# Input stage of a hybrid decoder layer: order of the low weight parts, shared value weights, rows of triangular blocks dealt in turn

## The chip, the cores and the metric

The kernel runs on one core of a Trainium2 chip. The metric is the device time of one execution in microseconds. The core has a matrix engine (TensorE, PE in the profile, with PEld for its weight loads), a vector engine (VectorE, DVE), an activation engine (ScalarE, ACT), GpSimd (POOL), and a queue for DMA issues (SyncE, SP). Each engine executes its own list of instructions in order; semaphores tie the lists together.

## The reference

One layer on 1024 tokens of width 1024: a norm, an input projection, two mixers side by side (sparse attention, and a gated delta rule with 4 heads of 128), an output projection, a gated feed-forward part with a short convolution. The change lies in the delta-rule mixer's input:

```python
h = rmsnorm(x, norm_mix[l])
proj = h @ w_in[l]
q_nsa, kv_nsa, gate_nsa, qkv_gdn, z_gdn, b_gdn, a_gdn = jnp.split(proj, SPLIT_POINTS, axis=-1)
...
qkv = jax.nn.silu(causal_dwconv(qkv, conv_w))
q, k, v = jnp.split(qkv, 3, axis=-1)
...
a_mat = jnp.where(strict, jnp.einsum('nbhid,nbhjd->nbhij', kb, kc) * decay, 0.0)
eye = jnp.eye(c, dtype=jnp.float32)
rhs = jnp.concatenate([vb, kb * jnp.exp(gcum)[..., None]], axis=-1)
sol = lax.linalg.triangular_solve(a_mat + eye, rhs, left_side=True, lower=True, unit_diagonal=True)
```

The chunks have 64 tokens. All is in float32; the kernel keeps the accuracy in its matmuls by splitting each operand in a high and a low part and adding three products: high by high, high by low, low by high.

## The kernel before

**Projection.** The normed input lies transposed in SBUF as `hH` and `hL`, [128, 8, 1024] each: 8 slices k of the model width by 1024 tokens. `split_weight` loads a [128, 1024] weight (512 KB, L113), ACT copies the high part `w_h` (L116), POOL subtracts to get the low part `w_l` (L118). `proj_block` makes one block of 128 output columns by 512 tokens: for each k the three matmuls of `mm3`, `w_h` by `hH` (L126), `w_h` by `hL` (L127), `w_l` by `hH` (L128), 24 in all, into one of two result banks `proj_ps`. The page prints the operands with the moving one first, `proj_ps<-hH,w_l`.

**Convolution.** `conv_block(ct, b)` serves column block ct (0 to 3 queries, 4 to 7 keys, 8 to 11 values, one head each) and half b of the tokens. ACT copies the bank to `cv_raw` and, scaled by a tap, to `cv_acc`; VectorE adds the three other taps (L465); ACT takes a tanh, VectorE finishes the silu (L469), and a DMA stores 512 tokens to `d_kqv` (L470). The last three columns of half 0 are kept in `tail` for half 1 (L460, L457). The loop in `phase_in` runs ct 0 to 11 for half 0, then ct 0 to 11 for half 1, and each call splits its own weight: 24 splits.

**Triangular blocks.** For a pair p of 128-token tiles `gdn_pre` loads `kq` (512 KB in 1024 pieces of 512 B, L276), makes the Gram products `kk_ps` (L285) and stores the 32 by 32 diagonal blocks of the strictly triangular matrix to `d_blk` (L297). `gdn_blocks` loads all 32 blocks of the pair as `bb`, [128, 32, 32], with each block in four partitions (L342), and inverts them there on VectorE: a partition holds one block and 8 of the 32 rows of its solution, `zb`. In 31 steps a multiply (L348) and an add (L350) apply one column of the block to the first `na` of the 8 rows. Partition 4i + r holds rows 8r to 8r + 7; since the same instruction runs on all partitions, `na` must cover the partition with the most rows that have begun, and so is `min(8, j + 1)`. The result goes to `d_z` (L352) in pieces of 1 KB. `gdn_solve` reads it back in transposed order, four loads of 16 KB a tile (`Zx`, L365), and puts blocks together on TensorE. `gdn_scale`, `gdn_scan` (L408, L415, L419) and `gdn_out` (L437 to L445) follow per tile.

**What sets the order.** The code of the delta rule stands behind the convolution loop in the text but has a raised priority, and a scheduler merges it with the convolution blocks, the blocks of `z` (gate of the delta rule) and the compressed keys (`kc_ps`, L704) into one fixed list for each engine. A list is executed in order, SP's DMA issues too. About 430 us into the execution the input stage is over, and the attention and the feed-forward part follow.

Of the kernel before, what the change touches and what calls it, by code (L numbers as in the profile page):

```python
# [9 lines left out]
F32 = mybir.dt.float32  # L10
# [8 lines left out]
P = 128  # L19
# [3 lines left out]
NK = DM // P  # L23
# [23 lines left out]
def shape_constants():  # L47
# [10 lines left out]
    c[:, C_DM:C_DM + 64] = j[:, None] == np.arange(64)[None, :]  # L58
    rho = i % 4
    for a in range(8):  # L60
        c[i, C_ZI + a * 32 + 8 * rho + a] = 1.0
    k = np.arange(P)
# [128 lines left out]
def proj_block(K, w, b):  # L191

    wh, wl = w
    ps = K.pp.tile([P, 512], F32, name="proj_ps", tag="proj")
    d = slice(b * 512, (b + 1) * 512)
    mm3(K.nc, ps, [(wh[:, k * P:(k + 1) * P], wl[:, k * P:(k + 1) * P], K.hH[:, k, d], K.hL[:, k, d])
                   for k in range(NK)])
    return ps
# [138 lines left out]
def gdn_blocks(K, p):  # L337

    nc = K.nc
    db, dz = K.d_blk[p % 2], K.d_z[p % 2]  # L340
    bb = K.gt.tile([P, 32, 32], F32, name="bb", tag="bb")
    nc.sync.dma_start(bb, bc(db.rearrange("t b h j i -> (t b h) j i"), 1, 4))  # L342
    z = K.gt.tile([P, 8, 32], F32, name="zb", tag="zb")
    nc.vector.tensor_copy(z, K.zinit)
    for j in range(31):
        na, n = min(8, j + 1), 31 - j
        tmp = K.gt.tile([P, 8, 32], F32, name="ztmp", tag="ztmp", bufs=1)
# [3 lines left out]
                                op=ALU.add)  # L351
    nc.sync.dma_start(dz.rearrange("t b h (r a) i -> (t b h r) (a i)", a=8), z.rearrange("p a i -> p (a i)"))  # L352


def gdn_solve(K, t, st):

    nc = K.nc
    B, wq, keg, vv = st.B, st.wq, st.keg, st.vv
    dz = K.d_z[t // 2 % 2][t % 2]
    Z, zt, qs = K.Zx[t % 2], K.zt, K.qs  # L360
    for c in range(2):
        nc.gpsimd.memset(Z[64 * c:64 * c + 32, :, 64 * c + 32:64 * c + 64], 0.0)
    for b in range(4):
        d = slice(32 * b, 32 * b + 32)
        nc.sync.dma_start(Z[d, :, d], dz[b].rearrange("h r i -> r h i"))  # L365

# [80 lines left out]

def conv_block(K, ct, b):

    nc = K.nc  # L450
    which, h = ct // 4, ct % 4
    ps = proj_block(K, split_weight(K, K.A["w_gdn"][ct]), b)
    raw = K.scr.tile([P, 3 + 512], F32, name="cv_raw", tag="cv_raw")
# [55 lines left out]
def phase_in(K, ctx):  # L509
# [45 lines left out]
    with ExitStack() as st:  # L555
# [15 lines left out]
        for b in range(2):  # L571
            gdn_gates(K, b)
        for ct in range(12):
            conv_block(K, ct, 0)
        for ct in range(12):
            conv_block(K, ct, 1)
        cp = mk("cmp", 1)
# [842 lines left out]
def open_common(K, ctx):  # L1420
# [35 lines left out]
    K.d_blk = [dp.tile([2, 4, 4, 32, 32], F32, name=f"d_blk{i}") for i in range(2)]  # L1456
    K.d_z = [dp.tile([2, 4, 4, 32, 32], F32, name=f"d_z{i}") for i in range(2)]

# [88 lines left out]
```

## Time and profile before

| | us |
|---|---|
| median of three runs | 1500.3 (1497.18, 1500.30, 1500.89) |
| the profiled execution | 1502.3 |
| its span in the trace | 1500.5 |
| TensorE busy | 1420.9 (95%) |
| VectorE busy | 1153.7 (77%) |
| ScalarE busy | 723.3 (48%) |
| GpSimd busy | 575.3 (38%) |

The span is what the trace covers; 1.8 us of the execution lie outside it. The share of busy time is an average over stages with different limits. Busy time of TensorE is modelled at its ends, so it is read beside the clock that the chip granted: 1.00 is 2.4 GHz, and a stretch with a mean below it spent part of its time at the lower level of 1.2 GHz. In groups of instructions the two numbers behind the bar are busy us and mean ns of one; behind the next bar stands how long the engine sat idle just before them, and what ended it. Groups are shown by the line that issued them.

### The profile page before, as it was taken

Reading aid. Unit: us, or ns where it says so; the run is one execution under the profiler, and the core shown is the slowest. Engines: PE = TensorE matmul, PEld = TensorE weight load, DVE = VectorE, ACT = ScalarE, POOL = GpSimd, SP = SyncE. Lnnn points to the kernel's source line nnn. Section 1 sums busy time; section 2 is a strip of 40 time slices with the busy share of each in tenths; the row PEclk is TensorE's granted clock in tenths of the full one; section 3 lists DMA queues with packets and bytes.
Section 4 is the critical chain, followed back from the end, with each engine's and each line's share of the span. In section 5 each row is a group of like instructions: output and inputs, shape, how many; then the busy total and the mean of one; then the engine's idle time right before and its main releaser. Section 6 shows DMA issues by size and latency. Waiting matters only on the chain.

```text
span 1500.5 us, 21074 instructions
## 1 busy us (share of the span) xinstructions
PE 1420.9 (95%) x7260; PEld 1163.8 (78%) x7260; DVE 1153.7 (77%) x2222; ACT 723.3 (48%) x1405; POOL 575.3 (38%) x567
## 2 busy tenths in 40 slices
PE   8998899999989999989998979999999999989997
PEld 8876677787877777777787858888888888778886
DVE  5768997886335788898975797888888888687656
ACT  7443343232233566788865544444444445333333
POOL 3355433344352245466563541111111112364444
PEclk9999999999999999999999989999999999999999
DMA  6245352444366543132215112323222235773333
GB/s 234 87 156 177 107 169 72 125 121 150 93 219 173 161 138 112 58 85 52 55 64 200 40 70 105 105 105 106 105 94 98 97 105 194 268 267 87 103 106 147
DMA packets 106059, 188.04 MB, mean 125 GB/s; under 512 B 17216, under 2 KB 52064, under 8 KB 105952
## 3 DMA queue, kind: packets, MB, share of 16 engines
q1 hardware_dynamic: 105952, 186.69, 38.5%
q8 instruction: 57, 0.93, 0.3%
q14 instruction: 50, 0.41, 0.1%
HBM read 135.00 MB, written 51.66 MB: 124 GB/s over the span
## 4 chain that ended last, share of the span: by engine, by line
PE 64%; DVE 19%; DMA 6%; ACT 4%; issue 4%; POOL 2%; SPq 1%; DVEq 0%; ACTq 0%; POOLq 0%
PE up_ps L1130 27%; PE dn_ps L1328 11%; PE proj_ps L128 3%; PE proj_ps L126 3%; PE proj_ps L127 3%; DVE cv_acc L465 3%; PE pt L880 2%; DVE pl L890 2%; PE po L892 1%; DVE zb L350 1%; PE po L891 1%; DVE ztmp L348 1%; PE s_ps L820 1%; PE s_ps L415 1%; DMA d_x<-og 1%
## 5 line engine op out<-in xcount | busy, mean ns | idle before, releaser
L1328 PE MATMUL dn_ps<-d_op 128*128 128x512 f32 x924 | 211.4, 390 | 5.7 <-DVE d_op L1322 3.8
L1328 PEld LDWEIGHTS dn_ps<-d_op 128*128 128x128 f32 x924 | 173.0, 188 | 43.6 <-DVE d_op L1322 5.0
L128 PE MATMUL proj_ps<-hH,w_l 128*128 128x512 f32 x384 | 158.3, 412 | 6.6 <-POOL w_l L118 6.6
L126 PE MATMUL proj_ps<-hH,w_h 128*128 128x512 f32 x384 | 156.2, 408 | 5.0 <-ACT cv_acc L463 3.2
L127 PE MATMUL proj_ps<-hL,w_h 128*128 128x512 f32 x384 | 155.3, 405 | 0.1
L1320 POOL TENSOR_TENSOR d_op<-a_raw,d_op 128x1024 fp32r<-128x1024 f32 (+1 forms) x42 | 104.7, 2496 | 123.0 <-ACT d_op L1319 105.6
L1130 PE MATMUL up_ps<-th,op_h 128*128 128x512 f32 x336 | 133.5, 398 | 7.1 <-ACT op_h L1154 7.1
L1130 PE MATMUL up_ps<-th,op_l 128*128 128x512 f32 x336 | 133.6, 398 | 3.6 <-DVE op_l L1156 3.6
L1130 PE MATMUL up_ps<-tl,op_h 128*128 128x512 f32 x336 | 133.3, 397 | 0.0
L118 POOL TENSOR_TENSOR w_l<-w_raw,w_h 128x1024 fp32r<-128x1024 f32 (+2 forms) x46 | 110.1, 2398 | 46.1 <-ACT w_h L116 44.5
L1322 DVE TENSOR_TENSOR d_op<-b,d_op 128x1024 fp32r<-128x1024 f32 (+1 forms) x42 | 80.8, 1928 | 48.5 <-ACT d_op L1321 42.1
L1130 PE MATMUL up_ps<-dl,op_h 128*128 128x512 f32 x288 | 113.8, 395 | 0.0
L1130 PE MATMUL up_ps<-dh,op_h 128*128 128x512 f32 x288 | 112.6, 395 | 1.0 <-ACT acc L167 1.0
L1130 PE MATMUL up_ps<-dh,op_l 128*128 128x512 f32 x288 | 110.5, 394 | 0.0
L882 ACT ACTIVATE ph<-pt 128x512 fp32r<-128x512 f32 (+1 forms) x148 | 85.3, 591 | 49.1 <-PE pt L880 41.3
L1242 DVE SCALAR_TENSOR_TENSOR ga<-f_g,vec,ga 128x1024 f32<-128x1024 f32 x44 | 89.3, 2029 | 16.9 <-ACT ga L1240 16.3
L890 DVE TENSOR_TENSOR pl<-pt,ph 128x512 fp32r<-128x512 f32 x132 | 89.5, 683 | 9.1 <-ACT ph L882 8.6
L128 PEld LDWEIGHTS proj_ps<-hH,w_l 128*128 128x128 f32 x384 | 74.6, 194 | 26.9 <-POOL w_l L118 10.6
L1154 ACT ACTIVATE op_h<-w_raw 128x1024 fp32r<-128x1024 f32 (+1 forms) x64 | 59.0, 923 | 74.8 <-PE up_ps L1130 69.7
L1319 ACT ACTIVATE d_op<-a_raw 128x1024 fp32r<-128x1024 f32 (+1 forms) x42 | 41.4, 988 | 108.7 <-PE dn_ps L1328 53.8
L1175 POOL MEMSET f_u<- 128x2 f32 x22 | 2.2, 100 | 234.0 <-DVE acc L1242 233.1
L126 PEld LDWEIGHTS proj_ps<-hH,w_h 128*128 128x128 f32 x384 | 74.6, 195 | 21.2 <-ACT cv_acc L463 4.9
(343 smaller groups left out, 3654.6 us busy)
## 6 DMA issues: line engine op xcount, KB each, us to landing
w_raw<-in_w_up_dram SPq DMA_DIRECT2D x44, 512.0 KB, 3.2
a_raw<-d_a SPq DMA_DIRECT2D x35, 512.0 KB, 3.6
w_raw<-in_w_gdn_dram SPq DMA_DIRECT2D x24, 512.0 KB, 3.5
d_a<-ga SPq DMA_DIRECT2D x44, 256.0 KB, 2.0
b<-in_w_down_dram SPq DMA_DIRECT2D x20, 512.0 KB, 6.9
d_a<-so SPq DMA_DIRECT2D x33, 256.0 KB, 2.0
qT<-d_q SPq DMA_DIRECT2D x32, 256.0 KB, 4.8
mg<-d_mix SPq DMA_DIRECT2D x16, 512.0 KB, 3.7
```

What stands on the lines that cost most here:

```text
L118: (low or nc.gpsimd).tensor_tensor(out=wl, in0=raw, in1=wh.bitcast(F32), op=ALU.subtract)
L126: nc.tensor.matmul(out, ah, bh, start=(i == 0), stop=False)
L127: nc.tensor.matmul(out, ah, bl, start=False, stop=False)
L128: nc.tensor.matmul(out, al, bh, start=False, stop=(i == n - 1))
L882: nc.scalar.activation(ph[0:kk], pt[0:kk], AF.Copy)
L890: nc.vector.tensor_tensor(out=pl, in0=pt, in1=ph.bitcast(F32), op=ALU.subtract)
L1130: mm = lambda a, b, start, stop: nc.tensor.matmul(out, a, b, start=start, stop=stop, skip_group_check=not first)
L1154: nc.scalar.activation(h, src, AF.Copy)
L1242: nc.vector.scalar_tensor_tensor(out=a, in0=raw[:, j:j + SEQ], scalar=tap(j), in1=a, op0=ALU.mult, op1=ALU.add)
L1320: nc.gpsimd.tensor_tensor(out=al, in0=raw, in1=ah.bitcast(F32), op=ALU.subtract)
L1322: nc.vector.tensor_tensor(out=bl, in0=b[js.start], in1=bh.bitcast(F32), op=ALU.subtract)
L1328: one = lambda a, b, start, stop: nc.tensor.matmul(ps, a, b, start=start, stop=stop, skip_group_check=not first)
```

## The change

1. `proj_block` no longer calls `mm3`. It issues the 16 matmuls with `w_h` first (`hH`, `hL` for each k in turn) and the 8 with `w_l` last, all from one line (L199).
2. `conv_block` gets the split weight. The loop now runs queries and keys of half 0, then the values of both halves with one split for the two, then queries and keys of half 1: 20 splits in place of 24.
3. In the triangular blocks partition 32r + i (r = 0 to 3) holds block i and rows r, r + 4, r + 8, ... of its solution, so `na` is `j // 4 + 1`. The initial values (C_ZI) follow this, `bb` is loaded by four DMAs of 32 partitions, and `d_z` has the rows first, [32, 2, 4, 4, 32], so that its store has pieces of 128 B. The loads of `Zx` have the same pieces as before.

```diff
-    rho = i % 4
+    rho = i // 32
     for a in range(8):
-        c[i, C_ZI + a * 32 + 8 * rho + a] = 1.0
+        c[i, C_ZI + a * 32 + 4 * a + rho] = 1.0
...
-    mm3(K.nc, ps, [(wh[:, k * P:(k + 1) * P], wl[:, k * P:(k + 1) * P], K.hH[:, k, d], K.hL[:, k, d])
-                   for k in range(NK)])
+
+    jobs = [(wh, h, k) for k in range(NK) for h in (K.hH, K.hL)] + [(wl, K.hH, k) for k in range(NK)]
+    for n, (w, h, k) in enumerate(jobs):
+        K.nc.tensor.matmul(ps, w[:, k * P:(k + 1) * P], h[:, k, d], start=(n == 0), stop=(n == len(jobs) - 1))
...
-    nc.sync.dma_start(bb, bc(db.rearrange("t b h j i -> (t b h) j i"), 1, 4))
+    for r in range(4):
+        nc.sync.dma_start(bb[32 * r:32 * r + 32], db.rearrange("t b h j i -> (t b h) j i"))
...
-        na, n = min(8, j + 1), 31 - j
+        na, n = j // 4 + 1, 31 - j
...
-    nc.sync.dma_start(dz.rearrange("t b h (r a) i -> (t b h r) (a i)", a=8), z.rearrange("p a i -> p (a i)"))
+    nc.sync.dma_start(dz.rearrange("(a r) t b h i -> (r t b h) a i", r=4), z)
...
-    dz = K.d_z[t // 2 % 2][t % 2]
+    dz = K.d_z[t // 2 % 2][:, t % 2]
...
-        nc.sync.dma_start(Z[d, :, d], dz[b].rearrange("h r i -> r h i"))
+        nc.sync.dma_start(Z[d, :, d], dz[:, b])
...
-def conv_block(K, ct, b):
+def conv_block(K, ct, b, w):
...
-    ps = proj_block(K, split_weight(K, K.A["w_gdn"][ct]), b)
+    ps = proj_block(K, w, b)
...
-        for ct in range(12):
-            conv_block(K, ct, 0)
-        for ct in range(12):
-            conv_block(K, ct, 1)
+
+        for cts, bs in ((range(8), (0,)), (range(8, 12), (0, 1)), (range(8), (1,))):
+            for ct in cts:
+                w = split_weight(K, A["w_gdn"][ct], low=None)
+                for b in bs:
+                    conv_block(K, ct, b, w)
...
-    K.d_z = [dp.tile([2, 4, 4, 32, 32], F32, name=f"d_z{i}") for i in range(2)]
+    K.d_z = [dp.tile([32, 2, 4, 4, 32], F32, name=f"d_z{i}") for i in range(2)]
```

On the engines' lists the change shows so. From the start of the attention on, the lists of all engines are the same before and after. Line numbers behind L199 are some 2 to 5 higher in the changed kernel.

TensorE at the compressed keys, before. `kc_ps` is the key product, `proj_ps` the block of another projection that fills in, `ot_ps` the output transposes, `s_ps` the state product of the scan, for which VectorE makes `vn`; x4 is four in a row.

```order
L408 MATMUL m_ps<-S,wq 128x128 x2
L704 MATMUL kc_ps<-cmp_x,w_4040 64x128
L126 MATMUL proj_ps<-hH,w_h 128x512
L127 MATMUL proj_ps<-hL,w_h 128x512
L437 MATMUL ot_ps<-ident,vv 128x128 x4
L415 MATMUL s_ps<-vn,kt 128x128 x4
L419 MATMUL o_ps<-vn,ab 128x128 x4
L704 MATMUL kc_ps<-cmp_x,w_4040 64x128
L128 MATMUL proj_ps<-hH,w_l 128x512
```

The same place after; six more pairs of `proj_ps` stand where the row of dots is.

```order
L411 MATMUL m_ps<-S,wq 128x128
L709 MATMUL kc_ps<-cmp_x,w_4028 64x128
L199 MATMUL proj_ps<-hH,w_h 128x512
L199 MATMUL proj_ps<-hL,w_h 128x512
...
L440 MATMUL ot_ps<-ident,vv 128x128 x4
L199 MATMUL proj_ps<-hH,w_h 128x512
L199 MATMUL proj_ps<-hL,w_h 128x512
L440 MATMUL ot_ps<-ident,vv 128x128 x4
L418 MATMUL s_ps<-vn,kt 128x128 x4
L422 MATMUL o_ps<-vn,ab 128x128 x4
L709 MATMUL kc_ps<-cmp_x,w_4028 64x128
L199 MATMUL proj_ps<-hH,w_l 128x512 x2
```

All 16 high-part matmuls of the block now stand between the first key product and `s_ps`, where two stood; the low-part ones come behind.

GpSimd about the end of the convolution's first half, before (`tail` and `cv_raw` are the three kept columns, `wq` and `sm` belong to the delta rule).

```order
L460 COPY tail<-cv_raw 128x3
L455 MEMSET cv_raw 128x3
L118 TENSOR_TENSOR w_l<-w_raw,w_h 128x1024
L460 COPY tail<-cv_raw 128x3
L455 MEMSET cv_raw 128x3
L333 TENSOR_TENSOR wq<-kq,gb 128x4x128
L118 TENSOR_TENSOR w_l<-w_raw,w_h 128x1024
L460 COPY tail<-cv_raw 128x3
L455 MEMSET cv_raw 128x3
L323 TENSOR_TENSOR sm<-sm,phalf 128x4
L118 TENSOR_TENSOR w_l<-w_raw,w_h 128x1024
```

The same place after.

```order
L463 COPY tail<-cv_raw 128x3 x2
L460 COPY cv_raw<-tail 128x3
L458 MEMSET cv_raw 128x3
L335 TENSOR_TENSOR wq<-kq,gb 128x4x128
L118 TENSOR_TENSOR w_l<-w_raw,w_h 128x1024
L335 TENSOR_TENSOR wq<-kq,gb 128x4x128
L325 TENSOR_TENSOR sm<-sm,phalf 128x4
L463 COPY tail<-cv_raw 128x3
L460 COPY cv_raw<-tail 128x3
L403 TENSOR_TENSOR ab<-at,cst 128x512
L335 TENSOR_TENSOR wq<-kq,gb 128x4x128
...
L118 TENSOR_TENSOR w_l<-w_raw,w_h 128x1024
```

One subtraction now serves two value blocks, and work of the delta rule stands between the subtractions.

SyncE's issues about the end of the convolution, before, from the last weight of the convolution (`in_w_gdn`); `kq_2578` and `kq_2605` are the loads of two tiles of the second half, `vT` one of values.

```order
L113 DMA w_raw_1765<-in_w_gdn_dram 128x1024
L113 DMA w_raw_1811<-in_w_z_dram 128x1024
L276 DMA kq_2578<-d_kqv_88 128x8x128
L470 DMA d_kqv_88<-cv_th_1675 128x512
L113 DMA w_raw_1875<-in_w_z_dram 128x1024
L317 DMA vT_2462<-d_kqv_88 128x4x128
L470 DMA d_kqv_88<-cv_th_1718 128x512
L113 DMA w_raw_1939<-in_w_z_dram 128x1024
L470 DMA d_kqv_88<-cv_th_1761 128x512
L276 DMA kq_2605<-d_kqv_88 128x8x128
```

The same place after (the rows ahead are stores and weights).

```order
L319 DMA vT_2444<-d_kqv_88 128x4x128
L473 DMA d_kqv_88<-cv_th_1694 128x512
L113 DMA w_raw_1915<-in_w_z_dram 128x1024
L473 DMA d_kqv_88<-cv_th_1737 128x512
L113 DMA w_raw_1979<-in_w_z_dram 128x1024
L319 DMA vT_2743<-d_kqv_88 128x4x128
L473 DMA d_kqv_88<-cv_th_1780 128x512
L278 DMA kq_2560<-d_kqv_88 128x8x128
L278 DMA kq_2587<-d_kqv_88 128x8x128
L509 DMA d_z_act_90<-z_th_1818 128x512
```

The first `kq` of the second half stood three stores ahead of the last `d_kqv`; now both stand behind it. Next on this list come the solution's store and eight loads of `Zx`.

## Rows read from the trace of the kernel before

**Rows 1.** The page, busy us of each engine, share, and number of instructions.

```profile
PE 1420.9 (95%) x7260; PEld 1163.8 (78%) x7260; DVE 1153.7 (77%) x2222; ACT 723.3 (48%) x1405; POOL 575.3 (38%) x567
```

**Rows 2.** Stretches of the span, with their length, busy time, and granted clock.

```profile
core 0: us, PE busy (x) PEld busy (x) DVE busy (x) ACT busy (x) POOL busy (x), PEclk, DMA share, GB/s
70.00:95.00 25.00, 25.00 (x110) 20.20 (x110) 16.42 (x17) 10.95 (x21) 12.28 (x12) 1.00 0.36 121
95.00:150.00 55.00, 49.29 (x221) 37.63 (x220) 44.50 (x78) 22.71 (x46) 32.42 (x29) 0.94 0.57 179
150.00:215.00 65.00, 59.02 (x301) 45.66 (x300) 61.85 (x150) 25.96 (x55) 26.69 (x20) 0.95 0.42 130
215.00:350.00 135.00, 131.84 (x916) 108.22 (x915) 108.94 (x330) 43.98 (x125) 47.81 (x47) 1.00 0.41 120
350.00:360.00 10.00, 7.50 (x30) 6.01 (x30) 7.08 (x14) 4.56 (x15) 7.84 (x8) 0.67 0.49 136
```

**Rows 3.** TensorE by lines, 95 to 215 us: count, busy, mean, idle before.

```profile
L128 PE MATMUL proj_ps<-hH,w_l 128*128 128x512 f32 x126 | 53.7, 426 | 6.6 <-POOL w_l L118 6.6
L126 PE MATMUL proj_ps<-hH,w_h 128*128 128x512 f32 x126 | 52.2, 415 | 3.2 <-ACT cv_acc L463 3.2
L127 PE MATMUL proj_ps<-hL,w_h 128*128 128x512 f32 x126 | 51.5, 408 | 0.0
```

**Rows 4.** TensorE in order of time: start us, us, instruction, idle before.

```profile
138.16 0.71 PE L128 MATMUL proj_ps<-hH,w_l 128*128 128x512 f32 x1 [2.13 <-POOL w_l L118]
138.67 0.63 PE L126 MATMUL proj_ps<-hH,w_h 128*128 128x512 f32 x1
139.10 0.63 PE L127 MATMUL proj_ps<-hL,w_h 128*128 128x512 f32 x1
```

**Rows 5.** VectorE in order of time, a held and an undisturbed instruction.

```profile
141.83 2.49 DVE L348 TENSOR_TENSOR ztmp<-zb,bb 128x112 f32<-128x112 f32 x1
...
144.88 0.74 DVE L465 SCALAR_TENSOR_TENSOR cv_acc<-cv_raw,vec,cv_acc 128x512 f32<-128x512 f32 x1
```

**Rows 6.** GpSimd in order of time at the same place.

```profile
141.79 2.39 POOL L118 TENSOR_TENSOR w_l<-w_raw,w_h 128x1024 fp32r<-128x1024 f32 x1 [1.97 <-ACT w_h L116]
```

**Rows 7.** VectorE by lines, 95 to 215 us, columns as in the third group.

```profile
L465 DVE SCALAR_TENSOR_TENSOR cv_acc<-cv_raw,vec,cv_acc 128x512 f32<-128x512 f32 x48 | 50.9, 1061 | 7.9 <-ACT cv_acc L463 6.0 <-POOL wq L333 1.4
L348 DVE TENSOR_TENSOR ztmp<-zb,bb 128x112 f32<-128x112 f32 (+29 forms) x43 | 21.2, 493 | 0.5
L350 DVE TENSOR_TENSOR zb<-zb,ztmp 128x112 f32<-128x112 f32 (+29 forms) x42 | 18.6, 442 | 0.7
```

**Rows 8.** GpSimd's subtraction, 95 to 215 us: shortest, median, longest ns; starts.

```profile
L118 POOL TENSOR_TENSOR w_l<-w_raw,w_h x16: 2347/2396/2943, 96.6 to 210.6; 128x1024 fp32r<-128x1024 f32 x16
```

**Rows 9.** VectorE by lines and shapes, 135 to 350 us.

```profile
L348 DVE TENSOR_TENSOR ztmp<-zb,bb 128x192 f32<-128x192 f32 x4 | 1.4, 355 | 0.0
...
L348 DVE TENSOR_TENSOR ztmp<-zb,bb 128x8 f32<-128x8 f32 x4 | 0.7, 171 | 0.1
```

**Rows 10.** DMA issues, 95 to 235 us: size of one, median us to landing.

```profile
d_kqv<-cv_th SPq DMA_DIRECT2D x18, 256.0 KB, 2.2
kq<-d_kqv SPq DMA_DIRECT2D x6, 512.0 KB, 5.5
...
d_blk<-B SPq DMA_DIRECT2D x16, 16.0 KB, 1.7
d_z<-zb SPq DMA_DIRECT2D x2, 128.0 KB, 2.8
```

**Rows 11.** TensorE in order of time at the compressed keys.

```profile
349.98 0.60 PE L437 MATMUL ot_ps<-ident,vv 128*128 128x128 f32 x4
353.08 1.88 PE L415 MATMUL s_ps<-vn,kt 64*128 64x128 f32 x8 [2.50 <-DVE vn L409]
```

**Rows 12.** The stores of the convolution: issue ns, first and last start.

```profile
L470 SPq DMA_DIRECT2D d_kqv<-cv_th x24: 319/320/433, 53.9 to 224.2; - x24
```

**Rows 13.** TensorE in order of time, the Gram products of the fifth tile.

```profile
232.36 1.09 PE L285 MATMUL kk_ps<-kq 128*64 128x128 f32 x16
```

## The prediction

> **What bounds the kernel now.** The first view is the page: TensorE is busy 95% of the span and VectorE 77% [rows 1], so a microsecond counts only where TensorE stands or runs at the lower of its two clock levels. Next is the order of instructions of the two kernels. From about 430 us on it is the same on every engine (the last 4700 of 6763 TensorE and 1461 of 2224 VectorE instructions), so only the input stage can move. The third view is the table by stretches [rows 2]. From 70 to 95 us 110 matmuls fill 25.00 us without a gap at a granted clock of 1.00, which is 0.227 us for one of 512 columns. From 95 to 215 us, where convolution blocks, triangular blocks and weight splits lie together, TensorE is busy 49.29 of 55 and 59.02 of 65 us, at a clock of 0.94 and 0.95. There VectorE is busy 61.85 of 65 us: in that part it is the fullest engine. From 215 to 350 us TensorE is busy 131.84 of 135 at 1.00, and little is left to win.
>
> The groups of lines of 95 to 215 us name what TensorE waits for [rows 3]: 6.6 us ahead of matmuls with low parts, for w_l on GpSimd, and 3.2 us ahead of the first matmuls of a block, for the convolution's copy cv_acc. One such place in order of time [rows 4]: a low-part matmul starts at 138.16 after 2.13 us of waiting, and the next starts, 138.67 and 139.10, lie 0.43 us apart, about twice 0.227: the wait is followed by the level of 1.2 GHz. What holds w_l and VectorE is seen in two timelines: a multiply of 112 elements takes 2.49 us from 141.83 [rows 5], and beside it a w_l runs 2.39 us from 141.79 [rows 6]. The same shape takes 0.28 us elsewhere by the size rule below, so VectorE is held for about the length of the GpSimd subtraction.
>
> **The convolution stretch, 95 to 215 us.** TensorE's need is 378 projection matmuls (126 in each of three groups [rows 3]) by 0.227, that is 85.8 us, and 522 − 378 = 144 others [rows 2]. These cost 9.8 us by the sixteen Gram matmuls that take 1.09 us [rows 13] and 16 us by what is left of the busy time (49.29 + 59.02, less 85.8, less the clock's shortfall of 0.06 x 55 + 0.05 x 65 = 6.5). So TensorE needs 96 to 102 of these 120 us; 18 to 24 is the most that can be had here.
>
> The change works on this in three ways. First, with low parts last, w_l is due 16 matmuls (3.6 us) after the first one of a block and not two (0.45 us) after it; the wait of 2.13 us in [rows 4] fits in that. Second, four of 24 weight loads, ACT copies and subtractions go, since a value weight serves both halves. Third, the triangular blocks have 1560 instead of 3156 elements for each of their two operations in a solve of 62 instructions. One multiply takes 355 ns for 192 elements and 171 ns for 8 [rows 9], so 1 ns an element and some 163 ns fixed; 2 x 1596 elements are 3.2 us a solve. In this stretch 85 of 248 such instructions run (43 + 42 [rows 7]), 1.4 solves or 4.4 us.
>
> The worth of a subtraction that is gone: the convolution's taps take a mean of 1061 ns [rows 7] beside 0.74 us for an undisturbed one [rows 5], which is 48 x 0.32 = 15 us of being held, and the triangular instructions a mean of 468 ns beside 263 by the size rule (mean 100 elements), 85 x 0.2 = 17 us. These 32 us go with POOL's 59.1 busy us of the stretch [rows 2], of which w_l has 16 x 2.4 = 38.4 [rows 8]: by its share 21 us for 16, or 1.3 each, and 4 x 1.3 = 5.2 us. VectorE's busy 106.4 us [rows 2] thus become 96.8; at the same share (0.887 of 120) the stretch takes 109 us, a gain of 11. From TensorE's side the named losses are 6.6 + 3.2 + 6.5 = 16. I take **13**, nearer to VectorE's number, because VectorE is the fuller engine; the ends are 5 (only w_l's own wait goes, and some of it comes back as a wait for cv_acc) and 22 (TensorE unbroken).
>
> On this the Trainium skill has a rule (SBUF — State Buffer, section "Who interferes with whom"): a VectorE operation with two inputs in SBUF and a GpSimd operation that reads SBUF lock each other out for the whole of the one that started first. The 2.49 beside 2.39 us of [rows 5, 6] agree. By that rule alone each subtraction that is gone could free up to its full 2.4 us, 9.6 in place of 5.2, and VectorE's side would give 16 and not 11; the sum stays at 13, since the measured hold is an average over subtractions that met no such operation.
>
> **The compressed-key place, 350 to 360 us.** TensorE waits 2.50 us ahead of the scan's state product, for VectorE's vn [rows 11], and then runs at 0.67 [rows 2]: 2.5 + 0.33 x 10 = 5.8 us. Before, two high-part matmuls stand between the key product and that point; now sixteen do, 14 x 0.227 = 3.2 us of work that needs nothing of VectorE. It covers the gap. I take 3, the ends being 0 and 5.8, because the held VectorE instruction itself stays.
>
> **Triangular blocks after 215 us.** The other 2.6 solves free 8.4 us of VectorE, but TensorE is busy 131.84 of 135 us there. I take 0, at most 3.
>
> **Moved and added transfers.** The store of the solution goes from 128 pieces of 1 KB to 1024 of 128 B. Such a store takes 2.8 us now; bounds are 1.7 (a store of 16 KB in pieces of 128 B) and 5.5 (a load of 1024 pieces of 512 B) [rows 10], so −1.1 to +2.7 a solve, −4 to +11 in four if nothing hid any of it. Other work stands beside the loads that wait for it, so I take +1, with ends −1 and +6. The block matrix now comes in four issues; three more at 0.32 us each (as the issues of [rows 12]) stand on SyncE's queue, 1 us a solve, ahead of other loads: 0, at most 2 in all. Four weight loads fewer free that queue as much.
>
> **Order of the halves.** The query and key blocks of the second half now come last, so the load kq for its first tile, which stood among the value blocks, stands behind the last store d_kqv; on SyncE the next kq, the store of the solution and its eight loads are queued behind it, and TensorE's Gram product waits in order with everything behind it. The last d_kqv is issued at 224.2 [rows 12]; 2.2 for it and 5.5 for kq [rows 10] give 231.9, and the Gram matmuls start at 232.36 now [rows 13]. So it just fits where both ends move up together; I take 0, at most +5 to +10.
>
> **Sum.** −13 − 3 + 0 + 1 + 0 = −15. The profiled execution took 1502.3 us (span 1500.5, 1.8 outside it), which gives 1487.3; it is 2.0 above the median of 1500.3, so **1485 us**.
>
> **Rivals.**
> (a) TensorE sets the pace of the whole stretch: VectorE's relief is enough, all of 18 to 24 comes, and the compressed-key place gives 5. 1500.3 − 22 − 5 + 1 = 1474. For it: three of the four named losses go at once. Against: 96.8 us of VectorE work in a stretch of 98 would leave it almost no idle time, and each block's chain runs through VectorE.
> (b) The wait for w_l is replaced by one for cv_acc: two result banks alternate, and a bank is free only when ACT has copied it, which itself waits for VectorE's taps. The gain is the 5 of the lower end: 1495. For it: the 3.2 us of such waits there now, and 7.9 us of VectorE idle time ahead of its taps, 6.0 of it for that copy [rows 7].
> (c) The small pieces: each solution store takes as much longer as the load of 1024 pieces, or doubles, and each of four is waited for in full: 1500.3 − 13 − 3 + 4 x 2.8 = 1495.5. For it: the pieces are an eighth as large. Against: the 16 KB stores with 128 B pieces land in 1.7 us. The Trainium skill (DMA: Bandwidth & Descriptors, "Specifications") says that pieces under 512 B are read and rewritten and miss the line rate; the trace of before has no 128 KB store of such pieces, and if that doubles 2.8 us, it is this rival.
> (d) Slower: the load kq arrives late. It decides once the last d_kqv moves up by less than TensorE does: then TensorE stands ahead of the Gram product, SyncE's queue holds the solution store and its loads behind two kq (2 x 5.5 = 11 us), and the clock falls to the lower level behind the stand (0.33 x 11 = 3.6). With a gain of 4 kept in the stretch: 1500.3 − 4 − 3 + 1 + 11 + 3.6 = 1509. For it: a margin of 0.4 us. Against: the end of the convolution is what the relief of VectorE moves.
> That the change does not do what it says is excluded for the counts: 24 weight loads became 20, and 3156 elements 1560.
>
> **How the numbers follow.** Forecast 0.62 (1478 to 1492 by its own ends), (a) 0.17, (b) 0.08, (c) 0.06, (d) 0.07. The range 1473 to 1497 holds the forecast, (b), (c) and about two thirds of (a), and leaves out (d). A measurement of this kernel can tell some 0.3% (4.5 us) from no change: faster is below 1495.8, which is the forecast, (a) and half of (b) and (c), 0.86; same 0.08; slower than 1504.8 is most of (d), 0.06.
>
> **What would show it.** In the changed kernel's profile: no wait of TensorE for w_l between 95 and 215 us (6.6 before); last convolution matmul about 13 us sooner; taps nearer 740 ns; a clock nearer 1.00 in the stretch; the stand before the state product at the compressed keys gone; a solution store of at most 5.5 us. I am wrong if TensorE's idle time ahead of proj_ps turns up under cv_acc in the same size, if the Gram product of the fifth tile waits for kq, or if the back-to-back work after the input stage begins less than 8 us sooner.

## The result

The changed kernel took 1486.3 us (median of 1484.88, 1485.35, 1487.33, 1489.42), the kernel before 1498.7 (four runs); the ratio is 0.9919 with a 95% interval of 0.9896 to 0.9943, so 12.1 us less, 8.5 to 15.6. Forecast were 1485 us and a gain of 15. The profiled execution took 1484.88 us, its span is 1483.1.

The total came out as forecast; the terms of the sum did not. First the stretches of the changed kernel, as in [rows 2], with the same columns, and two further ones:

```profile
70.00:95.00 25.00, 25.00 (x115) 20.32 (x114) 17.47 (x17) 12.46 (x22) 14.24 (x13) 1.00 0.37 127
95.00:150.00 55.00, 54.04 (x270) 42.84 (x269) 45.81 (x100) 20.58 (x45) 25.35 (x26) 1.00 0.52 160
150.00:215.00 65.00, 54.50 (x287) 43.18 (x287) 62.59 (x159) 25.73 (x52) 25.13 (x20) 0.96 0.40 123
215.00:350.00 135.00, 132.40 (x911) 108.83 (x910) 96.25 (x307) 43.69 (x124) 47.89 (x47) 0.99 0.42 118
350.00:360.00 10.00, 10.00 (x66) 7.66 (x65) 6.73 (x15) 4.38 (x17) 8.83 (x8) 1.00 0.54 182
390.00:430.00 40.00, 37.29 (x217) 31.70 (x216) 17.45 (x31) 17.44 (x44) 21.78 (x18) 1.00 0.68 212
```

From 95 to 150 us TensorE is now nearly full at 1.00. From 150 to 215 it is *less* busy than before, 54.50 against 59.02 of 65, and VectorE stands at 62.59: the limit named in the prediction is still there. At the compressed keys the stand and the low clock are gone.

The waits for the low part are gone too. TensorE by lines, 95 to 215 us, as [rows 3]; "issue" is time in which it waited for nothing that the profile shows:

```profile
L199 PE MATMUL proj_ps<-hH,w_h 128*128 128x512 f32 x132 | 52.5, 398 | 0.0
L199 PE MATMUL proj_ps<-hL,w_h 128*128 128x512 f32 x132 | 51.8, 393 | 0.0
L199 PE MATMUL proj_ps<-hH,w_l 128*128 128x512 f32 x130 | 34.9, 403 | 0.0
L287 PE MATMUL kk_ps<-kq 128*64 128x128 f32 x64 | 5.3, 316 | 2.6 <-issue 2.6
L256 PE MATMUL tr_ps<-ident,kq 128*128 128x128 f32 x24 | 3.8, 279 | 4.4 <-DVE at L301 2.0 <-DVE vv L333 1.7 <-ACT junk L307 0.8
L256 PE MATMUL tr_ps<-ident,vT 128*128 128x128 f32 x8 | 1.3, 283 | 2.6 <-DVE kt L330 1.6 <-issue 1.0
```

In place of the 9.8 us in front of the projections there are now 2.6 us in front of the Gram products and 7.0 in front of transposes, 5.3 of these for VectorE. The waits have moved to instructions of the delta rule, and their sum is nearly what it was. The stretch from 95 us to the Gram products of the fifth tile, before and then after, holds the same number of matmuls:

```profile
95.00:232.40 137.40, 124.07 (x619) 94.84 (x617) 123.10 (x270) 55.15 (x111) 62.87 (x52) 0.95 0.48 151
95.00:225.70 130.70, 119.24 (x619) 93.57 (x617) 115.00 (x280) 50.33 (x104) 51.53 (x47) 0.97 0.46 141
```

TensorE is idle for 13.3 us before and 11.5 after. So of the 6.7 us that this stretch became shorter, only 1.9 are idle time; the other 4.8 are busy time of as many matmuls, an estimated 3 of them from the mean clock of 0.97 in place of 0.95.

How much time each place gave is read from when a TensorE instruction with the same role starts in both traces (us in the profiled executions):

| first start of | before | after | gain so far | forecast so far |
|---|---|---|---|---|
| Gram products, fifth tile | 232.4 | 225.7 | 6.7 | 13 |
| ninth state product of the scan | 341.9 | 336.4 | 5.5 | 13 |
| eleventh, behind the compressed keys | 368.5 | 360.1 | 8.4 | 16 |
| compressed values (`vc_ps`) | 411.2 | 397.7 | 13.5 | 16 |
| last matmul | 1490.9 | 1473.2 | 17.7 | 15 |

The two profiled executions lie 17.4 us apart, more than the medians (12.4). So the convolution stretch gave half of the forecast, and the part from 342 to 411 us 8 us where 3 were forecast. The last 4.2 us of the table fall for the most part where the lists are the same, and are about what the two executions lie further apart than the medians; no part of the change accounts for them.

### The profile page after: what moved, and what is told of

It reads as the page before. It is cut to its first block, busy times and chain, and to the rows that moved or that the text cites. A ratio compares the mean times of both kernels' runs of the same rounds, so it can differ in the third digit from the quotient of the medians.

```text
span 1483.1 us, 21069 instructions
## 1 busy us (share of the span) xinstructions
PE 1408.9 (95%) x7260; PEld 1154.7 (78%) x7260; DVE 1140.0 (77%) x2222; ACT 721.6 (49%) x1401; POOL 564.9 (38%) x563
## 4 chain that ended last, share of the span: by engine, by line
PE 68%; DVE 18%; DMA 6%; issue 3%; ACT 3%; POOL 1%; SPq 1%; DVEq 0%; ACTq 0%; POOLq 0%
PE up_ps L1135 27%; PE proj_ps L199 12%; PE dn_ps L1333 10%; PE pt L885 2%; DVE cv_acc L468 2%; DVE pl L895 2%; DMA b<-in_w_down_dram 2%; PE po L897 1%; PE s_ps L825 1%; PE po L896 1%; PE s_ps L418 1%; PE s_ps L827 1%; DMA a_raw<-d_a 1%; PE m_ps L411 1%; PE og_ps L126 1%
## 5 line engine op out<-in xcount | busy, mean ns | idle before, releaser
L1333 PE MATMUL dn_ps<-d_op 128*128 128x512 f32 x924 | 212.8, 392 | 5.8 <-DVE d_op L1327 4.1
L199 PE MATMUL proj_ps<-hH,w_h 128*128 128x512 f32 x384 | 152.1, 398 | 0.3 <-ACT hH L187 0.3
L199 PE MATMUL proj_ps<-hL,w_h 128*128 128x512 f32 x384 | 151.1, 395 | 0.1
L118 POOL TENSOR_TENSOR w_l<-w_raw,w_h 128x1024 fp32r<-128x1024 f32 (+2 forms) x42 | 100.0, 2387 | 29.0 <-ACT w_h L116 15.5
L199 PE MATMUL proj_ps<-hH,w_l 128*128 128x512 f32 x384 | 103.1, 402 | 0.0
L1247 DVE SCALAR_TENSOR_TENSOR ga<-f_g,vec,ga 128x1024 f32<-128x1024 f32 x44 | 89.2, 2028 | 16.9 <-ACT ga L1245 16.3
L199 PEld LDWEIGHTS proj_ps<-hH,w_h 128*128 128x128 f32 x384 | 71.9, 188 | 15.9 <-issue 0.8
L199 PEld LDWEIGHTS proj_ps<-hL,w_h 128*128 128x128 f32 x384 | 72.0, 188 | 15.0 <-DVE hL L188 0.5
```

The source lines that it names most:

```text
L118: (low or nc.gpsimd).tensor_tensor(out=wl, in0=raw, in1=wh.bitcast(F32), op=ALU.subtract)
L199: K.nc.tensor.matmul(ps, w[:, k * P:(k + 1) * P], h[:, k, d], start=(n == 0), stop=(n == len(jobs) - 1))
L1247: nc.vector.scalar_tensor_tensor(out=a, in0=raw[:, j:j + SEQ], scalar=tap(j), in1=a, op0=ALU.mult, op1=ALU.add)
L1333: one = lambda a, b, start, stop: nc.tensor.matmul(ps, a, b, start=start, stop=stop, skip_group_check=not first)
```

## The experiments

Twelve kernels ran, each compared with the kernel before on the same chip. Differences are (ratio − 1) x 1498.7 us, with the interval. The two theories in the expectations: **W** is the prediction's (waits for the low part and the clock behind them); **V** says that VectorE's queue sets the pace and that GpSimd's subtractions keep it full by holding its instructions.

| run | what it is | us against before | interval | Gram, fifth tile |
|---|---|---|---|---|
| a | low parts last, alone | +1.6 | −0.9 to +4.0 | 228.4 |
| b | values shared, alone | −9.4 | −11.4 to −7.5 | 227.0 |
| c | rows dealt, alone | −3.3 | −4.9 to −1.6 | 231.6 |
| e | change without low parts last | −11.1 | −14.4 to −7.6 | 224.9 |
| f | change without dealt rows | −12.0 | −16.2 to −7.9 | 229.8 |
| j | order of b, but 24 splits | +0.1 | −2.1 to +2.5 | 232.5 |
| i | change, subtraction twice | +19.6 | +16.3 to +23.1 | 258.3 |
| g | before, low parts on VectorE | −15.6 | −19.3 to −12.0 | 220.5 |
| d | change, low parts on VectorE | −19.6 | −22.0 to −17.4 | 212.8 |
| h | as d, without low parts last | −20.1 | −24.0 to −16.0 | 220.2 |
| k | shared values and low parts on VectorE | −16.9 | −19.2 to −14.8 | 218.6 |
| l | as d, and the four gate weights | −20.2 | −22.9 to −17.5 | 215.5 |

### Each part alone (a, b, c)

Run a changes only the matmuls of a block:

```diff
-    mm3(K.nc, ps, [(wh[:, k * P:(k + 1) * P], wl[:, k * P:(k + 1) * P], K.hH[:, k, d], K.hL[:, k, d])
-                   for k in range(NK)])
+    jobs = [(wh, h, k) for k in range(NK) for h in (K.hH, K.hL)] + [(wl, K.hH, k) for k in range(NK)]
...
```

> Only the order of the 24 matmuls of a projection block is changed (low parts last); splits, loop and triangular blocks as before. Theory V (between 140 us and the Gram products of the fifth tile, at 232.4 us before, VectorE's queue sets the pace, so that a wait of TensorE taken away there comes back as another): the fifth tile's Gram products move by 3 us at most, and the gain comes from the compressed keys on, some 9 us by the end of the input stage; total 7 to 11 us. Theory W, that of the prediction (the waits for the low part and the clock behind them are what costs time there): no wait for the low part, the fifth tile's Gram products 6 to 10 us sooner, 3 us more at the compressed keys; total 9 to 13 us.

Measured: nothing, +1.6 us (−0.9 to +4.0). Here are TensorE's waits in it from 95 to 232 us: who waited for whom, us in total, times, longest.

```profile
PE kk_ps L287 <- issue: 3.0, 1, 3.0
PE q_ps L374 <- DVE zt L372: 2.7, 1, 2.7
PE tr_ps L256 <- issue: 2.4, 1, 2.4
PE proj_ps L199 <- POOL w_l L118: 2.4, 1, 2.4
PE proj_ps L199 <- ACT cv_acc L465: 1.6, 2, 1.1
PE tr_ps L256 <- DVE ztmp L350: 1.5, 1, 1.5
PE nd_ps L272 <- DVE vv L333: 0.4, 1, 0.4
```

And the same view of the kernel before:

```profile
PE proj_ps L128 <- POOL w_l L118: 6.6, 8, 2.1
PE proj_ps L126 <- ACT cv_acc L463: 3.2, 3, 1.4
PE m_ps L408 <- DVE wq L389: 1.3, 1, 1.3
PE x_ps L380 <- issue: 1.0, 1, 1.0
PE tr_ps L254 <- DVE at L299: 0.6, 1, 0.6
PE tr_ps L254 <- issue: 0.3, 1, 0.3
PE kk_ps L285 <- issue: 0.2, 1, 0.2
```

The sums are 13.2 us before and 14.0 in run a. The wait for the low part went from 6.6 to 2.4, the one for cv_acc from 3.2 to 1.6, and the transposes, the Gram products and the solve wait for the difference. As an account of the total W falls. The Gram products of the fifth tile do come 4.0 us sooner, a microsecond more than V allowed, but those of the sixth come later (241.6 against 240.6), and V's second half, a gain from the compressed keys on, is wrong for this kernel: the compressed values start at 416.7, 5.5 us later than before. There it pays new waits, among them 2.24 us for `vn` in front of a state product at 233.10. Its fixed list of instructions is another one, and what stands at a given place is no longer comparable by itself.

Run b is the loop and the argument of `conv_block` alone:

```diff
-        for ct in range(12):
-            conv_block(K, ct, 0)
-        for ct in range(12):
-            conv_block(K, ct, 1)
+        for cts, bs in ((range(8), (0,)), (range(8, 12), (0, 1)), (range(8), (1,))):
+            for ct in cts:
+                w = split_weight(K, A["w_gdn"][ct], low=None)
+                for b in bs:
+                    conv_block(K, ct, b, w)
```

> Only the loop is changed: the values of both halves share a split, 20 splits in place of 24. Theory V: of the four subtractions that go, two or three stood in the full stretch of VectorE, and each held it for some 2.1 us: the fifth tile's Gram products 3 to 6 us sooner, total 2 to 6 us. Theory W: 1.3 us for each that goes, 5 us at most there, and part of it stays hidden; total 0 to 4 us. Should the later load of the second half's keys and queries show, the Gram products wait for it and the kernel is slower by up to 9 us.

Measured: −9.4 us, above both theories; 5.4 of it by the fifth tile's Gram products. The late load of the second half's keys and queries does not show. The one wait for such a load from 95 to 320 us is this:

```profile
PE kk_ps L285 <- DMA kq<-d_kqv: 0.5, 1, 0.5
```

It stands at 108.3 us, ahead of first-half Gram products. The fifth tile's own load landed at 225.9 us, and its Gram products start at 227.0 without a wait.

The 5.4 us go with four subtractions fewer ahead of these products, 13 against 17 from 95 us on. More came at the compressed keys: the eleventh state product starts 11.6 us sooner than before (356.9). In this run's list of VectorE `vn` stands ahead of an instruction that is held there, so that TensorE has no wait for it:

```profile
342.17 0.69 DVE L409 TENSOR_TENSOR vn<-vv,m_ps 64x512 f32<-64x512 f32 x1
342.89 2.26 DVE L697 TENSOR_SCALAR cmp_t<-cmp_t 128x128 f32<-128x128 f32 x1
```

Run c is the third part (constants, four loads, `na = j // 4 + 1`, layout of `d_z`):

```diff
-        na, n = min(8, j + 1), 31 - j
+        na, n = j // 4 + 1, 31 - j
...
```

> Only the triangular blocks are changed (rows dealt in turn, four loads of the block matrix, store in pieces of 128 B). Theory V: two solves lie ahead of the fifth tile's Gram products, 3.2 us of VectorE each: they come 4 to 6 us sooner; the other two solves lie beside a full TensorE and give nothing; total 3 to 6 us. Theory W: 1.4 solves in the stretch, 4.4 us of VectorE, of which TensorE's waits for the low part let about half through; total 1 to 3 us. The waits at the compressed keys (2.50 us) stay by both.

Measured: −3.3 us, inside V's range and just above W's, but only 0.8 by the Gram products where V said 4 to 6. TensorE waits for the low part as before (6.7 us) and VectorE's share from 150 to 215 us is the same, 61.53 of 65. So some 6 us of multiplies and adds taken from VectorE's queue ahead of that point (two solves at 3.0) bought less than one. Neither theory predicted that.

The three add up to −11.1, and the change measured −12.1.

### Two at a time (e, f)

```diff
 # e: the change with proj_block as before
-    for n, (w, h, k) in enumerate(jobs):
...
+    mm3(K.nc, ps, [(wh[:, k * P:(k + 1) * P], wl[:, k * P:(k + 1) * P], K.hH[:, k, d], K.hL[:, k, d])
...
 # f: the change with the triangular blocks as before
-        na, n = j // 4 + 1, 31 - j
+        na, n = min(8, j + 1), 31 - j
```

> The changed kernel without its first part: the 24 matmuls of a projection block alternate as before; shared values and dealt rows stay. Alone the order gave 1500.0 (nothing), shared values 1488.6 and dealt rows 1495.4, so that the sum of the three is 13.5 us of the 12.4 measured together. If the parts add up, the order is worth nothing here too: 1485 to 1488. Rival, that the order has its worth only once VectorE has been relieved by the other two: 1489 to 1493, and the waits for the low part (6.6 us before) are back.

Measured: −11.1 us (1487.6 on the scale of 1498.7; its own median 1488.2 stood beside 1501.1 for the kernel before). Without the order of the matmuls the change is worth the same within the intervals, and TensorE's waits from 95 to 232 us hold none for the low part, though the order is the old one. The rival falls.

> The changed kernel without its third part: rows of the triangular blocks as before; order and shared values stay. If the parts add up (order 0, values 10): 1488 to 1490, as the shared values alone. If the order costs something wherever VectorE is full and dealt rows pay for it: 1491 to 1495. If dealt rows are worth more behind the other two (each solve of 62 instructions shortens a queue that is then the only limit): 1490 to 1493 as well, but with VectorE's share above 0.95 in 150 to 215 us.

Measured: −12.0 us, which is 1486.7 on the same scale; VectorE's share from 150 to 215 us is 61.41 of 65. That is below each of the expected ranges: the dealt rows add nothing that can be measured to the other two. The shared values alone (−9.4) are most of the change; whether the order and the dealt rows add 1 or 3 us together the intervals do not tell.

### Why shared values are worth so much (j, i)

Run j keeps the order of blocks of run b and the 24 splits of the kernel before:

```diff
             for ct in cts:
-                w = split_weight(K, A["w_gdn"][ct], low=None)
                 for b in bs:
+                    w = split_weight(K, A["w_gdn"][ct], low=None)
                     conv_block(K, ct, b, w)
```

> The kernel before with the changed kernel's order of the convolution blocks (values of both halves one behind the other, queries and keys of the second half last), but with a split for each block, 24 as before. Shared values gave 10 us. If the four subtractions that go are the cause (theory V): the gain is gone, 1495 to 1502. If it is the order of the blocks (values of the second half early, so that the second half's scaling has its data sooner): 1488 to 1491, as with shared values.

Measured: +0.1 us, Gram products at 232.5 as before (232.4). The wait of 2.50 us for `vn` at the compressed keys is there as before. The order of blocks is worth nothing by itself; the 9 us come with the four splits that go, 5.5 of them by the fifth tile's Gram products (227.0 in run b). A split is a load, a copy on ACT and a subtraction on GpSimd, and run i doubles the last alone:

```diff
-    (low or nc.gpsimd).tensor_tensor(out=wl, in0=raw, in1=wh.bitcast(F32), op=ALU.subtract)
+    for _ in range(2 if twice else 1):
+        (low or nc.gpsimd).tensor_tensor(out=wl, in0=raw, in1=wh.bitcast(F32), op=ALU.subtract)
```

> The changed kernel with the subtraction of the 20 convolution weights on GpSimd issued twice, the second writing the same values again; nothing else. If a subtraction costs by holding VectorE (theory V), 20 more hold it 1.6 us each; some 13 of them lie between 95 and 215 us: 15 to 25 us slower than the changed kernel (1486.3), taps back at over 1.1 us, and the fifth tile's Gram products 12 to 20 us later. If what matters is only when the low part is there (theory W): it comes 2.4 us later, 16 matmuls at 0.227 give 3.6 us of room, so 0 to 6 us slower. If GpSimd has time to spare, nothing.

Measured: 31.7 us slower than the changed kernel, 1.6 us for each of 20 subtractions, beyond V's range and far beyond W's. The fifth tile's Gram products start 32.6 us later. The taps take 1063 ns (40 to 430 us; 943 in the changed kernel), a little less than the 1.1 us expected. TensorE waits for no low part in it either; by lines from 95 to 215 us it waits for VectorE's and ACT's results:

```profile
L200 PE MATMUL proj_ps<-hH,w_h 128*128 128x512 f32 x121 | 49.1, 405 | 3.6 <-ACT cv_acc L467 3.6
L200 PE MATMUL proj_ps<-hH,w_l 128*128 128x512 f32 x121 | 34.8, 429 | 0.0
L288 PE MATMUL kk_ps<-kq 128*64 128x128 f32 x64 | 5.3, 315 | 7.1 <-issue 6.7 <-DMA kq<-d_kqv 0.5
L257 PE MATMUL tr_ps<-ident,kq 128*128 128x128 f32 x20 | 3.9, 329 | 7.3 <-DVE at L302 7.1 <-ACT junk L308 0.2
```

Part of these 31.7 us may be the low part itself coming later, by a way that does not show as a wait of TensorE; the run does not separate that. That GpSimd's other work came late behind the added subtractions is a rival that the trace speaks against: from 95 us to the Gram products the waits of all engines for GpSimd come to 0.3 us.

How the subtraction holds VectorE is seen in the changed kernel as in [rows 5, 6]. VectorE, start us and us, then GpSimd:

```profile
145.54 0.24 DVE L353 TENSOR_TENSOR zb<-zb,ztmp 128x76 f32<-128x76 f32 x1
145.82 2.33 DVE L351 TENSOR_TENSOR ztmp<-zb,bb 128x72 f32<-128x72 f32 x1
148.18 0.23 DVE L353 TENSOR_TENSOR zb<-zb,ztmp 128x72 f32<-128x72 f32 x1
```

```profile
145.66 2.39 POOL L118 TENSOR_TENSOR w_l<-w_raw,w_h 128x1024 fp32r<-128x1024 f32 x1 [1.43 <-ACT w_h L116]
```

The instruction of 72 elements needs 0.23 us by its neighbours and takes 2.33. This is the rule and not an accident: the 16 subtractions of the kernel before between 95 and 215 us all lie beside a VectorE instruction of 1.5 to 2.9 us, 35.0 us in all; in the changed kernel 11 of 12 lie beside one of 2.0 to 2.8 us, 26.4 us. Undisturbed, the sixteen would take 7.7 us (seven taps at 0.74, nine triangular instructions by the prediction's size rule). The other 27 us, 1.7 for each subtraction, is time in which VectorE counts as busy beyond its own work.

### Taking the hold away (g, d, h, k, l)

The hold goes if VectorE does the subtraction itself. Run g makes this one edit in the kernel before, run d in the changed kernel:

```diff
 # g
-    ps = proj_block(K, split_weight(K, K.A["w_gdn"][ct]), b)
+    ps = proj_block(K, split_weight(K, K.A["w_gdn"][ct], low=K.nc.vector), b)
 # d
-                w = split_weight(K, A["w_gdn"][ct], low=None)
+                w = split_weight(K, A["w_gdn"][ct], low=nc.vector)
```

> The changed kernel with one edit: the low parts of the 20 convolution weights are subtracted on VectorE instead of GpSimd. Theory V with its mechanism: each subtraction on GpSimd holds a VectorE instruction for nearly its length, 2.3 us in place of 0.2 to 0.7, about 2.1 us; done on VectorE it costs 1.25 us (the same shape there in the feed-forward part takes 1.27). With nine of them in the full stretch: 0.85 x 9 = 7 to 8 us sooner at the fifth tile's Gram products than in the changed kernel, total 4 to 8 us below it. Rival: the hold fell in time that VectorE had to spare, so 20 x 1.25 = 25 us of new VectorE work lengthens its queue: 8 to 12 us later there, total above the changed kernel.

Measured: −19.6 us against before, 7.5 below the changed kernel, which is in V's range, and the fifth tile's Gram products 12.9 us sooner than there, more than V said; some 5 us of these are lost again behind them. The stretches of run d:

```profile
95.00:150.00 55.00, 55.00 (x278) 44.35 (x277) 45.72 (x108) 23.68 (x49) 14.99 (x21) 1.00 0.53 168
150.00:215.00 65.00, 63.74 (x364) 51.12 (x362) 60.49 (x180) 27.21 (x54) 13.65 (x14) 1.00 0.48 152
```

TensorE is busy 118.7 of 120 us at the upper clock level. VectorE is hardly less busy than before (60.49 of 65), but with work. By lines, 40 to 430 us (busy us, mean ns), the changed kernel, and then run d:

```profile
L468 DVE SCALAR_TENSOR_TENSOR cv_acc<-cv_raw,vec,cv_acc 128x512 f32<-128x512 f32 x72 | 67.9, 943 | 12.0 <-ACT cv_acc L466 11.0
L351 DVE TENSOR_TENSOR ztmp<-zb,bb 128x60 f32<-128x60 f32 (+24 forms) x124 | 43.9, 354 | 10.9 <-DMA bb<-d_blk 8.1
L353 DVE TENSOR_TENSOR zb<-zb,ztmp 128x60 f32<-128x60 f32 (+24 forms) x124 | 37.4, 301 | 2.5
L472 DVE SCALAR_TENSOR_TENSOR cv_th<-cv_th,cv_acc 128x512 f32<-128x512 f32 x24 | 22.3, 929 | 8.6 <-ACT cv_th L471 8.4
```

```profile
L468 DVE SCALAR_TENSOR_TENSOR cv_acc<-cv_raw,vec,cv_acc 128x512 f32<-128x512 f32 x72 | 58.0, 805 | 2.7 <-ACT cv_acc L466 1.7
L351 DVE TENSOR_TENSOR ztmp<-zb,bb 128x60 f32<-128x60 f32 (+24 forms) x124 | 34.6, 279 | 7.9 <-DMA bb<-d_blk 5.4
L353 DVE TENSOR_TENSOR zb<-zb,ztmp 128x60 f32<-128x60 f32 (+24 forms) x124 | 29.9, 241 | 2.8
L118 DVE TENSOR_TENSOR w_l<-w_raw,w_h 128x1024 fp32r<-128x1024 f32 x18 | 23.9, 1328 | 5.0 <-PE proj_ps L199 4.7 <-ACT w_h L116 0.3
L472 DVE SCALAR_TENSOR_TENSOR cv_th<-cv_th,cv_acc 128x512 f32<-128x512 f32 x24 | 16.9, 702 | 11.6 <-ACT cv_th L471 11.5
```

The four groups of other work fall from 171.5 to 139.4 us, 32.1 for the 18 subtractions moved in this stretch (two of the 20 stand ahead of it), 1.8 each; each then costs 1.33 us on VectorE itself. For this shape VectorE's own work is shorter than the hold.

> The kernel before with one edit: the low parts of its 24 convolution weights are subtracted on VectorE. In the changed kernel this edit gave 8.3 us; there 20 subtractions less on GpSimd took 32.1 us from the taps, silus and triangular instructions of VectorE (1.6 us each) and put 1.3 us each on it. If the hold is the cause in the kernel before too, 24 of them give 8 to 12 us: 1487 to 1491, taps at some 0.8 us in place of 1.06, and no wait of TensorE for a low part from GpSimd. If what gave the 8.3 us was only that the order of the changed kernel needs it, 1496 to 1501.

Measured: −15.6 us, more than expected and more than the whole change. The taps' mean is 814 ns (1058 before, same stretch); TensorE's waits from 95 to 232 us are 3.6 us in place of 13.2, none for a low part.

> Shared values, dealt rows, and low parts of the convolution weights on VectorE, but the matmuls of a block in the old order. If the order is worth nothing: 1477 to 1479, as with it (1478.0). If low parts last is what lets the subtraction stand late on VectorE's queue (behind taps of the block ahead), TensorE waits for the low part again, two matmuls after a block's start: 1480 to 1486.

Measured: −20.1 us, within 0.5 of run d. The order of the matmuls is worth nothing there either, and no wait for a low part showed.

> Two edits on the kernel before: shared values, and the convolution's low parts on VectorE. Neither the order of the matmuls nor the dealt rows. With both of these it was 1478.0, without the order 1479.5. If the hold is the cause and the dealt rows are worth little once VectorE is no longer full: 1478 to 1482. If dealt rows are worth their 12.8 us of VectorE work here: 1485 to 1491, hardly better than low parts on VectorE alone (1484.1).

Measured: −16.9 us (1481.9). It is 2.7 us above run d, with intervals that overlap, and 1.3 below run g. So where the convolution's subtractions hold nothing, shared values are worth about 1 us, not 9, and order and dealt rows together up to 3. This is what V says of the shared values: their worth was the subtractions.

> The changed kernel with the low parts of the convolution weights and of the four gate weights (z) on VectorE. With the convolution's alone it is 1478.0. Between 230 and 350 us TensorE is busy 117.4 of 120 us there, so that by theory V little can be won: 1476 to 1480. If the hold costs wherever VectorE stands in the scan's chain: 1470 to 1475.

Measured: −20.2 us, as run d within the interval; TensorE is busy 120.00 of 120 us from 95 to 215. With TensorE full in the stretch there is nothing more for VectorE to give. Runs d, h and l, at 1478 to 1480 us, beat both kernels.

One number holds through all fourteen traces: from 95 us to the fifth tile's Gram products VectorE is busy for 0.86 to 0.90 of the time, while the time itself runs from 117.8 us (run d) to 163.3 (run i). Runs g and i:

```profile
95.00:220.50 125.50, 121.84 (x614) 97.55 (x612) 111.67 (x268) 53.58 (x107) 33.24 (x34) 0.99 0.54 169
95.00:258.30 163.30, 134.43 (x650) 104.84 (x648) 144.62 (x286) 54.70 (x112) 87.74 (x64) 0.92 0.40 122
```

Against the kernel before, VectorE's busy time falls by 11.4 us in run g and the Gram products come 11.9 sooner; it grows by 21.5 in run i and they come 25.9 later. TensorE's share is not constant: 0.82 in run i, 0.97 in run g, and 0.98 to 1.00 in runs d, h, k and l, where TensorE is a limit as well. That is what V says, with held time counted as busy time.

## Why the prediction was right, and where it was not

- **What bounds the kernel.** Right: VectorE is the fullest engine from 150 to 215 us, and it stayed so. The prediction also saw that some 32 of VectorE's 106.4 busy us are held time; what it had wrong is how much of that the subtractions hold.
- **Low parts last.** Named as the first of three ways in which 13 us come; it was worth nothing that can be measured in runs a, e and h. The wait for the low part does not hang on it either: in run a 2.4 us of it are left, in run e, with the old order, none. The failing step is the sum from TensorE's side ("the named losses are 6.6 + 3.2 + 6.5 = 16"): a wait at an engine that is not the bound is where the bound shows, and it took other names.
- **Four subtractions fewer.** Right mechanism, and in the stretch nearly the right size: 5.2 us were forecast, and run b's fifth Gram products come 5.4 sooner. The other 4 of its 9.4 us came behind them, most of it at the compressed keys by that run's list, and no step priced that. The 1.3 us for each is low as an average, because the 32 us of held time were spread over everything that GpSimd does: read one by one, the sixteen subtractions hold 27 of them, 1.7 each. Moving frees 1.8 each (run d), doubling costs 1.6 us of kernel time each (run i). The Trainium skill (SBUF — State Buffer, section "Who interferes with whom") says that a VectorE operation with two inputs in SBUF contends with a GpSimd operation that reads SBUF, and calls this an exclusive lock; 2.33 beside 2.39 us in the changed kernel agrees again. The full 2.4 us for each, 9.6 in the prediction, is more than the measured average: many instructions meet only a part of a subtraction, as a tap of the kernel before that starts 1.1 us into one and takes 1.86 us.
- **Dealt rows.** Nearly all of the 3.2 us a solve is there (81.3 against 93.1 us in the two groups between 40 and 430 us, 3.0 for each of four), but it gave 0.8 us in the stretch alone, and nothing measurable beside the other parts. That 4.4 us of VectorE's work are worth 4.4 us of time there was the error. Which instruction of VectorE is the one that TensorE waits for was not followed up; it stays open.
- **Convolution stretch, 13 us.** 6.7 by the fifth tile's Gram products. The lower end, 5, was nearer. The step from VectorE's side (less busy time at the same share) nearly held: up to these products 123.10 us became 115.00, at a share of 0.90 and 0.88. Two signs fell short: the last convolution block's copy starts 9.8 us sooner (207.4 against 217.2), not 13, and the taps from 95 to 215 us take 862 ns (1061 before), not near 740, since the subtractions that are left still hold.
- **Compressed keys, 3 us.** The stand is covered, as [rows 11] said. The changed kernel's ot_ps and s_ps:

```profile
347.30 0.60 PE L440 MATMUL ot_ps<-ident,vv 128*128 128x128 f32 x4
348.20 0.60 PE L440 MATMUL ot_ps<-ident,vv 128*128 128x128 f32 x4
348.73 1.16 PE L418 MATMUL s_ps<-vn,kt 64*128 64x128 f32 x8
```

  No wait stands ahead of s_ps, where it was 2.50 us, and the clock is 1.00 from 340 to 360 us, where it was 0.67 from 350 on. The held VectorE instruction itself stays, as the prediction said:

```profile
343.94 2.46 DVE L700 TENSOR_SCALAR cmp_t<-cmp_t 128x128 f32<-128x128 f32 x1 [2.34 <-ACT cmp_t L699]
```

  The gain so far grows by 2.9 us up to the eleventh state product, as forecast. But the low parts last are not the only way to it: in runs b and e, with the old order, no such wait is there either, and in run k, also with the old order, it is back (2.44 us). Where the list puts `vn` decides it too.
- **Behind it, 0 us.** Here another 5 us came, from the eleventh state product up to the compressed values, that no step held. Before, TensorE was busy 35.13 of the 40 us from 390 on at a clock of 0.91, now 37.29 at 1.00:

```profile
390.00:430.00 40.00, 35.13 (x242) 30.46 (x241) 16.89 (x33) 12.71 (x37) 16.87 (x13) 0.91 0.50 156
```

  Run b has a clock of 0.87 and run e 0.91 there; f, with the low parts last, has 1.00 as the changed kernel does, but run a, with them too, 0.87. So this place hangs on the list that the whole makes, not on a part.
- **Transfers.** The store of the solution landed after 3.8 us (median of four, 95 to 350 us) and 3.1 before, inside the bounds. The Trainium skill (DMA: Bandwidth & Descriptors, "Specifications") says that pieces under 512 B miss the line rate; the doubling that the prediction estimated beside it did not come. Over all traces such medians run from 2.4 to 3.9 us with pieces of 128 B and from 1.8 to 3.5 with pieces of 1 KB, so that no cost of the small pieces shows. VectorE waited 8.1 us for the block matrix in the changed kernel, 1.9 before and 1.7 in run c; what the four loads have in that was not measured apart.
- **Rivals.** None was the case as stated. (b) came nearest: the waits came back, at the transposes and not under cv_acc, and the convolution stretch gave 6.7 us. (d), the late keys, made TensorE wait neither in run b nor in the changed kernel, where the load landed at 223.9 us and the Gram products start at 225.7. (a), a full TensorE, is what run d made of it, and by then the time was 1478.

So the sum was right by luck, because two errors of opposite sign met: the order of the matmuls and the dealt rows were priced in the convolution stretch, and are worth little there; the end of the input stage was priced at nothing, and gave 5 us.

## What to carry to other kernels

If an engine's busy share is high, look at the longest durations of its short instructions before counting its work: what is held counts as busy. If a wait goes away and the time stays, add up all waits of the stretch before and after; an equal sum under other names (13.2 and 14.0 us here) means that the bound is elsewhere. And price an operation by doubling it: the second subtraction said in one run what no row had shown plainly.

## What the runs showed of the hardware

Beside a GpSimd subtraction of 128 x 1024 values (2.4 us, two operands in SBUF) a VectorE instruction of 0.2 to 0.7 us nearly always took 1.5 to 2.9 us, 1.7 longer on average in the kernel before; the same subtraction on VectorE takes 1.22 to 1.33 us in runs d, g and k (means). Moving 24 of them from the engine with time to spare to the full one made the kernel before 15.6 us faster (12.0 to 19.3).
